# Neighbourhood attention inside a two-layer encoder trunk: a pipeline of tiles, stacked score products, value products of full width

## The chip, the cores and the metric

The kernel runs on one core of one Trainium2 chip. Its engines work side by side: TensorE (PE) multiplies matrices, with a separate record for its weight loads (PEld), VectorE (DVE), ScalarE (ACT) and GpSimd (POOL) work elementwise, and SyncE (SP) starts transfers between the chip's memory and the core. Every engine takes its instructions in the order in which the program lists them. The metric is the device time of one execution in microseconds (us), the median of the runs.

## The reference

The trunk has an even layer (neighbourhood attention beside a gated recurrence) and an odd layer (two other recurrences). Each makes an input projection, its mixers, and an output projection with a residual and a LayerNorm. 2048 tokens stand on a grid of 32 rows of 64. The change touches the attention: each token attends, in 8 heads of 64 channels, to a window of 8 rows and 16 columns.

```
s = jnp.einsum('brnqhd,brnkhd->brnhqk', qb, kg).astype(jnp.float32) * (dh ** -0.5) + bias[None]
s = jnp.where(valid[None, None, :, None], s, -jnp.inf)
p = jax.nn.softmax(s, axis=-1).astype(v.dtype)
o = jnp.einsum('brnhqk,brnkhd->brnqhd', p, vg)
...
ya = ya.reshape(bsz, seq, WIDTH_A) * jax.nn.silu(ag)
...
x = layer_norm(DEEPNORM_ALPHA * x + gate * y, ln_g[l], ln_b[l])
```

All is in 32-bit floats. Products that need the full precision are made of parts: a high part H in the short format (fp32r) and the remainder L, as H·H + H·L + L·H.

## The kernel before

The attention's work is cut into 16 blocks: `rg`, a group of 8 grid rows (512 tokens), by `hp`, a pair of heads. Each block has two heads, each head four tiles `n` of 16 grid columns, so there are 128 tiles of 128 queries. A tile's keys are 24 columns wide at the grid's edges and 32 inside, by 12 grid rows at the top and bottom groups and 16 else: 288, 384 or 512 keys.

`na_block` (L692) writes a block. It fetches q, k and gate for both heads (L702, L704, L706), a bias table for each head (`nat`, L711) and the values (`nav`, L716, one transfer for each of the four widths), and makes high and low parts of q and k (L721 to L724). Then for each head it writes four tiles of scores (three products, `nas`, L741; bias and row minimum on DVE, L744; exponential with row sum on ACT, L746), one reciprocal for the four tiles (L749), and four tiles of values: a scaling on POOL (L754), transposes on PE (`napt`, L757), a copy (`napts`, L760 or L762), and value products (`nay`, L764). At the end of the block comes the gating (`nayo`, L768) and a store.

Both heads of a block share tiles: head h has partitions 64h to 64h + 63 of q and k, so a score product uses 64 of the array's 128 rows; a value product takes 64 of the 128 columns of `nav` as its weights, and so fills 64 of the array's columns.

Around it stand other products. `units` (L1259) writes whole units of the input projection (`oak`, `oav`, `oag` at L204); the last of them are mixed with the first blocks. Then the pool of the input projection is closed, the output projection's weights are fetched, multiplied by a gate and split (`woraw`, `wo`, L783 to L786), and the other blocks alternate with tiles of the output projection (`OutProj.tile`, L826, products `oo` at L860: for each half of the columns and each of 8 chunks, yH·wH, yH·wL, yL·wH).

The final order on each engine is not that of the code: a scheduler simulates the program while it is built and places each instruction when it finds its engine free, by priority (the order of writing). So one engine's list can hold instructions of two or three blocks mixed. The SP queue is part of it: a transfer that waits for a free buffer holds those behind it.

Of the kernel before, what the change touches and what calls it, by code (L numbers as in the profile page):

```python
# [10 lines left out]
F32 = mybir.dt.float32  # L11
# [106 lines left out]
class InProj:  # L118
# [72 lines left out]
    def block(self, u, wh, wl, half, g, i):  # L191
# [4 lines left out]
        for d in range(ND):  # L196
            if u["kind"] == "ch":
                ops = ((wh[:, d, sl], hH[:, d, :]), (wh[:, d, sl], hL[:, d, :]), (wl[:, d, sl], hH[:, d, :]))
                oo = o
            else:  # L200
                ops = ((hH[:, d, sl], wh[:, d, :]), (hH[:, d, sl], wl[:, d, :]), (hL[:, d, sl], wh[:, d, :]))
                oo = o[:, :n]
            for m, (a, b) in enumerate(ops):
                nc.tensor.matmul(oo, a, b, start=d == 0 and m == 0, stop=d == ND - 1 and m == 2)  # L204
        if u["kind"] == "ch":
# [4 lines left out]
    def blocks(self, u, w, half, g):  # L210
        for i in range(u["n"] // P if u["kind"] == "ch" else 4):
            self.block(u, *w, half, g, i)
            yield

# [61 lines left out]
def run(g):  # L276
    for _ in g:
        pass

# [412 lines left out]
def na_block(e, pool, ps, bank, rg, hp, q_d, k_d, v_d, vcol, gate_d, tab_d, y_d):  # L692

    nc = e.nc
    nr = NA_NR[rg]
    nb = nr // 4
    ts_ = slice(rg * 512, (rg + 1) * 512)
    k0 = NA_R0[rg] * 64
    rt = NA_RT[rg]

    q = pool.tile([P, 512], F32, name="naq", tag="naq", bufs=1)
    nc.sync.dma_start(q, q_d[:, ts_])  # L702
    k = pool.tile([P, 1024], F32, name="nak", tag="nak", bufs=1)
    nc.sync.dma_start(k[:, :nr * 64], k_d[:, k0:k0 + nr * 64])  # L704
    gate = pool.tile([P, 512], F32, name="nag", tag="nag", bufs=2)
    nc.sync.dma_start(gate, gate_d[:, ts_])  # L706
    o0, o1 = NA_TOFF[rt, 0], NA_TOFF[rt, 2] + nr * 24
    tabs = []
    for h in range(2):
        t = pool.tile([P, 1280], F32, name="nat", tag="nat", bufs=2)  # L710
        nc.sync.dma_start(t[:, :o1 - o0], tab_d[2 * hp + h, :, o0:o1])  # L711
        tabs.append(t)
    vs = pool.tile([P, 4, 4, P], F32, name="nav", tag="nav", bufs=2)
    vt = v_d[k0:k0 + nr * 64, vcol:vcol + P].rearrange("(b x) d -> x b d", x=256)
    for n in range(4):
        nc.sync.dma_start(vs[:4 * NA_W[n], n, :nb, :], vt[4 * NA_C0[n]:4 * (NA_C0[n] + NA_W[n])])  # L716
    qH = pool.tile([P, 512], F32R, name="qH", tag="qH", bufs=2)
    qL = pool.tile([P, 512], F32R, name="qL", tag="qL", bufs=2)
    kH = pool.tile([P, 1024], F32R, name="kH", tag="kH", bufs=2)
    kL = pool.tile([P, 1024], F32R, name="kL", tag="kL", bufs=2)  # L720
    nc.scalar.copy(qH, q)  # L721
    nc.vector.tensor_sub(qL, q, qH.bitcast(F32))
    nc.scalar.copy(kH[:, :nr * 64], k[:, :nr * 64])
    nc.vector.tensor_sub(kL[:, :nr * 64], k[:, :nr * 64], kH[:, :nr * 64].bitcast(F32))  # L724
    kHv, kLv = (t.rearrange("p (b x) -> p b x", x=256) for t in (kH, kL))
    yp = ps.tile([P, 4, P], F32, name="nay", tag="nay", bufs=e.nay_bufs)
    for h in range(2):
        p0 = 64 * h
        sl = slice(p0, p0 + 64)
        mx = pool.tile([P, 4], F32, name="namx", tag="namx", bufs=3)  # L730
        sm = pool.tile([P, 4], F32, name="nasm", tag="nasm", bufs=3)
        pr = []
        for n in range(4):
            w = NA_W[n]
            nk = nr * w
            off = NA_TOFF[rt, NA_CT[n]] - o0
            sc = bank("nas")
            qs = slice(n * P, (n + 1) * P)
            ks = (slice(0, nb), slice(4 * NA_C0[n], 4 * (NA_C0[n] + w)))
# [3 lines left out]
            p = pool.tile([P, 512], F32, name="nap", tag="nap", bufs=e.nap_bufs)  # L743
            nc.vector.tensor_tensor_reduce(p[:, :nk], sc[:, :nk], tabs[h][:, off:off + nk], -1.0, 3.0e38,  # L744
                                           ALU.add, ALU.min, mx[:, n:n + 1])
            nc.scalar.activation(p[:, :nk], p[:, :nk], AF.Exp, bias=mx[:, n:n + 1], scale=-1.0,  # L746
                                 accum_out=sm[:, n:n + 1])
            pr.append(p)
        nc.vector.reciprocal(sm, sm)  # L749
        for n in range(4):  # L750
            w = NA_W[n]
            nk = nr * w
            p = pr[n]
            nc.gpsimd.tensor_tensor(p[:, :nk], p[:, :nk], sm[:, n:n + 1].broadcast_to([P, nk]), ALU.mult)  # L754
            pt = ps.tile([P, 4, P], F32, name="napt", tag="napt", bufs=e.napt_bufs)
            for b in range(nb):
                nc.tensor.transpose(pt[:4 * w, b, :], p[:, b * 4 * w:(b + 1) * 4 * w], e.ident)  # L757
# [801 lines left out]
```

## Time and profile before

| | |
|---|---|
| median of 3 runs | 2823.4 us (2813.05 to 2828.3) |
| the profiled execution | 2820.02 us |
| its span, first to last instruction | 2818.2 us |
| PE busy | 2584.9 us (92%) |
| DVE, ACT, POOL busy | 1510.3, 1095.2, 1327.7 us |
| mean granted PE clock | 0.951 |

The page gives busy time for each engine and the span in 40 slices of 70.5 us. A busy share counts an engine as busy while a product runs, whatever the clock; the granted clock is a row of its own (1.00 is 2.4 GHz, 0.50 is 1.2 GHz). Window tables cut the span where one likes, timelines list instructions with their start, and wait lists say whom an engine waited for.

### The profile page before, as it was taken

The numbers are of one execution on the slowest core, as the hardware profiler recorded it, in microseconds if no ns is written. First come the engines' busy times: TensorE is split into PE (matmuls) and PEld (weight loads), VectorE is DVE, ScalarE is ACT, GpSimd is POOL, SyncE is SP. The second block draws the span as 40 slices with busy tenths as digits, with TensorE's granted clock in tenths as the row PEclk, the third lists the DMA queues.
The fourth block names the chain that finished last, engine by engine and source line by source line (L and its number), as shares of the span: only waits on it lengthen the run. The fifth ranks groups of instructions, "written<-read, shape, count | busy, mean of one in ns | idle before, by whom it ended". The sixth has DMA issues, their size and how long they took to land. (4 is left out here: it accounts for less than half of the span.)

```text
span 2818.2 us, 53141 instructions
## 1 busy us (share of the span) xinstructions
PE 2584.9 (92%) x21112; PEld 2135.7 (76%) x21112; DVE 1510.3 (54%) x2463; ACT 1095.2 (39%) x2309; POOL 1327.7 (47%) x1289
## 2 busy tenths in 40 slices
PE   7988998988989999999898899999979988889998
PEld 5866778877778767777787777898777767767776
DVE  6255422144433355554546647333565479788886
ACT  3154412244434443433233334423334334655553
POOL 4253323343444243333356556334444577567775
PEclk9999999998999969999999999999999989989999
DMA  8424353322367554645456234443345655734341
GB/s 270 159 76 155 117 172 120 120 78 82 126 192 229 168 173 150 188 139 173 129 162 211 99 120 128 161 138 132 110 138 188 195 174 178 236 125 159 98 138 67
DMA packets 261000, 420.93 MB, mean 149 GB/s; under 512 B 21232, under 2 KB 138896, under 8 KB 260752
## 3 DMA queue, kind: packets, MB, share of 16 engines
q1 hardware_dynamic: 260752, 417.53, 45.9%
q8 instruction: 167, 2.74, 0.4%
q14 instruction: 81, 0.66, 0.1%
HBM read 285.07 MB, written 132.38 MB: 148 GB/s over the span
## 5 line engine op out<-in xcount | busy, mean ns | idle before, releaser
L186 POOL TENSOR_TENSOR wl<-wraw,wh 128x1024 fp32r<-128x1024 f32 (+2 forms) x116 | 292.1, 2535 | 447.6 <-ACT wh L185 436.5
L860 PE MATMUL oo<-wo,yH 128*128 128x512 f32 x1024 | 325.1, 404 | 5.8 <-ACT yH L844 3.3
L860 PEld LDWEIGHTS oo<-wo,yH 128*128 128x128 f32 x1024 | 191.8, 192 | 51.4 <-ACT yH L844 7.9
L754 POOL TENSOR_TENSOR nap<-nap,nasm 128x384 f32<-128x384 f32 (+2 forms) x128 | 115.7, 933 | 177.0 <-DVE nasm L749 175.2
L860 PE MATMUL oo<-wo,yL 128*128 128x512 f32 x512 | 197.9, 401 | 0.6 <-DVE yL L845 0.3
L463 POOL TENSOR_TENSOR Kp<-Kp,T 128x256 f32<-128x256 f32 x144 | 127.3, 889 | 116.1 <-ACT km L422 47.8
L185 ACT CAST wh<-wraw 128x1024 fp32r<-128x1024 f32 (+2 forms) x116 | 116.8, 1051 | 140.4 <-PE oak L204 19.9
L459 DVE TENSOR_TENSOR Q<-Q,T 128x512 f32<-128x512 f32 x144 | 146.0, 1015 | 1.2
L970 DVE SCALAR_TENSOR_TENSOR cva<-cvx,cw,cva 128x512 f32<-128x512 f32 x96 | 104.6, 1097 | 75.1 <-ACT cva L968 73.7
L461 DVE TENSOR_TENSOR Kp<-Kp,T 128x256 f32<-128x256 f32 x144 | 100.2, 696 | 63.8 <-PE l L449 28.9
L764 PE MATMUL nay<-napts,nav 128*64 128x128 f32 (+1 forms) x896 | 131.5, 295 | 1.0 <-ACT napts L762 1.0
L764 PEld LDWEIGHTS nay<-napts,nav 128*64 128x64 f32 (+1 forms) x896 | 103.3, 146 | 32.5 <-issue 22.1
L860 PEld LDWEIGHTS oo<-wo,yL 128*128 128x128 f32 x512 | 96.7, 189 | 25.3 <-DVE yL L845 3.0
L156 POOL TENSOR_TENSOR hL<-hf,hH 128x512 fp32r<-128x512 f32 x36 | 50.1, 1400 | 126.8 <-ACT hH L155 126.7
L746 ACT ACTIVATE nap<-nap,namx 128x384 f32<-128x384 f32 (+2 forms) x128 | 79.3, 620 | 64.9 <-DVE namx L744 63.9
L204 PE MATMUL ox<-hH,wh 128*128 128x512 f32 x256 | 103.5, 404 | 0.3 <-ACT st L310 0.3
L204 PE MATMUL ox<-hL,wh 128*128 128x512 f32 x256 | 103.6, 405 | 0.0
L204 PE MATMUL oqf<-hH,wh 128*128 128x512 f32 x256 | 103.0, 403 | 0.0
L204 PE MATMUL ox<-hH,wl 128*128 128x512 f32 x256 | 103.0, 402 | 0.0
L204 PE MATMUL oqf<-hH,wl 128*128 128x512 f32 x256 | 102.8, 402 | 0.0
L744 DVE CUSTOM_DVE_ANT_0 nap<-nas,nat 128x384 f32<-128x384 f32 (+2 forms) x128 | 70.5, 558 | 58.1 <-PE napt L757 29.9
L204 PE MATMUL oqf<-hL,wh 128*128 128x512 f32 x256 | 101.5, 397 | 0.0
(376 smaller groups left out, 7764.5 us busy)
## 6 DMA issues: line engine op xcount, KB each, us to landing
wraw<-in_o_w_dram SPq DMA_DIRECT2D x56, 512.0 KB
wraw<-in_e_w_dram SPq DMA_DIRECT2D x44, 512.0 KB
adw<-in_ada_w_dram SPq DMA_DIRECT2D x32, 512.0 KB
tk<-xtok SPq DMA_DIRECT2D x31, 384.0 KB
nat<-in_na_tab_dram SPq DMA_DIRECT2D x16, 640.0 KB
xt<-in_x_dram SPq DMA_DIRECT2D x16, 512.0 KB
adw<-in_ada_p_dram SPq DMA_DIRECT2D x16, 512.0 KB
r<-in_x_dram SPq DMA_DIRECT2D x16, 512.0 KB
```

Of the source, the lines that this page charges most:

```text
L185: nc.scalar.copy(h[:, sl], raw)
L186: (nc.vector if e.wl_dve else nc.gpsimd).tensor_sub(l[:, sl], raw, h[:, sl].bitcast(F32))
L204: nc.tensor.matmul(oo, a, b, start=d == 0 and m == 0, stop=d == ND - 1 and m == 2)
L459: nc.vector.tensor_tensor(qv, qv, view(tcur, toff + 1, [[nb - 1, 2], [2, n2], [0, s]]), ALU.mult)
L461: nc.vector.tensor_tensor(kv, kv, view(tcur, toff + nb + 1, [[2, n2], [0, s]]), ALU.mult)
L463: nc.gpsimd.tensor_tensor(kv, kv, view(tcur, toff, [[2, n2], [0, s]]), ALU.mult)
L744: nc.vector.tensor_tensor_reduce(p[:, :nk], sc[:, :nk], tabs[h][:, off:off + nk], -1.0, 3.0e38, ALU.add, ALU.min, mx[:, n:n + 1])
L746: nc.scalar.activation(p[:, :nk], p[:, :nk], AF.Exp, bias=mx[:, n:n + 1], scale=-1.0, accum_out=sm[:, n:n + 1])
L754: nc.gpsimd.tensor_tensor(p[:, :nk], p[:, :nk], sm[:, n:n + 1].broadcast_to([P, nk]), ALU.mult)
L764: nc.tensor.matmul(yp[sl, n, :], vs[:4 * w, n, b, p0:p0 + 64], pts[:4 * w, b, :], start=b == 0, stop=b == nb - 1, tile_position=(0, p0))
L860: nc.tensor.matmul(o, a[:, c, :], b[c][:, ns], start=c == order[0] and m == 0, stop=c == order[-1] and m == 2)
L970: nc.vector.scalar_tensor_tensor(acc, xr[:, k:k + SW], cw[:, i, k:k + 1], acc, ALU.mult, ALU.add)
```

## The change

`na_block` becomes a class `Na` whose `steps` is a generator. It runs over all 128 tiles; at step j it writes the scores of tile j, the transposes of tile j - 3 and the value products of tile j - 4, and yields after each. A head's q, k and table are fetched three tile steps ahead of its first scores. `weave` distributes n of these yields evenly over the steps of another generator: units of the input projection cut into steps of two chunks (`fine`), and output tiles cut into steps of two products (`OutProj.steps`).

For each head, q and k (64 channels) are fetched twice, into both halves of the partitions. `qS` holds the high part of q above and the low part below; with kH and kL, each twice, two products of 128 rows give (qH + qL)·kH + (qH + qL)·kL. The values' weights are all 128 columns of `nav`, both heads'; the half of the output that belongs to the other head is not read. Keys of the tiles with 24 columns and 16 rows are cut into three pieces of 128 instead of four of 96, and `nav` is fetched piece by piece. The reciprocal is made for each tile, the gating for each head. PSUM banks for scores go from 3 to 2, for `nay` from 1 to 2; `yH` of the output projection has 2 buffers in layer 1. Output products run with the low part's products last in each group of chunks, in both layers; in layer 1, for the last tiles of each group of four, both column halves alternate and the last chunk is fetched later (`across`).

```diff
-            for m, (a, b) in enumerate(((qH, kHv), (qH, kLv), (qL, kHv))):
-                nc.tensor.matmul(sc[:, :nk], a[sl, qs], b[sl, ks[0], ks[1]], start=m == 0, stop=m == 2,
-                                 tile_position=(p0, 0))
...
-            for b in range(nb):
-                nc.tensor.matmul(yp[sl, n, :], vs[:4 * w, n, b, p0:p0 + 64], pts[:4 * w, b, :],
-                                 start=b == 0, stop=b == nb - 1, tile_position=(0, p0))
...
+class Na:
+    LAG = (0, 3, 4)
...
+            w4 = 4 * NA_W[n]
+            kb = w4 if b.nb * w4 % P else P
+            b.kb.append(kb)
+            for j in range(b.nb * w4 // kb):
+                at = j * kb
+                while at < (j + 1) * kb:
+                    r, x = divmod(at, w4)
+                    m = min(w4 - x, (j + 1) * kb - at)
+                    nc.sync.dma_start(vs[at - j * kb:at - j * kb + m, n, j, :],
+                                      vt[4 * NA_C0[n] + x:4 * NA_C0[n] + x + m, r])
+                    at += m
...
+        for o in range(2):
+            os_ = slice(64 * o, 64 * o + 64)
+            nc.sync.dma_start(q[os_], b.q[hs, b.ts])
+            nc.sync.dma_start(k[os_, :nk], b.k[hs, b.ks])
...
+        nc.scalar.copy(s.q, q)
+        nc.vector.tensor_sub(s.q[64:], q[64:], s.q[64:].bitcast(F32))
+        nc.scalar.copy(kH[:, :nk], k[:, :nk])
+        nc.vector.tensor_sub(kL[:, :nk], k[:, :nk], kH[:, :nk].bitcast(F32))
...
+        for m, k in enumerate(s.k):
+            nc.tensor.matmul(sc[:, :nk], s.q[:, n * P:(n + 1) * P], k[:, :b.nb, 4 * NA_C0[n]:4 * (NA_C0[n] + w)],
+                             start=m == 0, stop=m == 1)
...
+        for j in range(nj):
+            nc.tensor.matmul(s.yp[:, n, :], b.vs[:kb, n, j, :], s.pts[n][:kb, j, :], start=j == 0, stop=j == nj - 1)
...
+        prods = [(c, m) for cs in (order[:cut], order[cut:]) for ms in ((0, 1), (2,)) for c in cs for m in ms]
...
-    units("ak1 ag0", 1)
-    na(3, 0)
-    units("av1", 1)
-    na(3, 1)
-    units("ag1", 1)
+    units("ag0", 1)
+    weave(na, 36, ip.fine(U["ak1"], 1), ip.fine(U["av1"], 1))
+    weave(na, 24, ip.fine(U["ag1"], 1))
...
-    for rg in (2, 1, 0):
-        for hp in range(4):
-            na(rg, hp)
-            op.tile(4 * (rg + 1) + 3 - hp)
+    for _ in range(36):
+        next(na)
+    for t in range(15, 4, -1):
+        weave(na, 24 if t > 7 else 32, (op.steps(t, *(((3, 4), False, None, True) if t % 4 == 3 else ())), 24))
+    run(na)
+    op.tile(4)
```

PE, among the products of the second output tile, before. Names: `nas` scores, `nay` values, `napt` transposes, `oo` output products; the last field is the output's size and how many stand in a row.

```order
L860 MATMUL oo<-wo_9655,yL 128x512
L741 MATMUL nas<-kH,qH 128x384
L741 MATMUL nas<-kL,qH 128x384
L741 MATMUL nas<-kH,qL 128x384
L764 MATMUL nay<-napts,nav 64x128 x8
L757 MATMUL napt<-c_ident,nap 128x128 x4
L757 MATMUL napt<-c_ident,nap 96x128 x4
L741 MATMUL nas<-kH,qH 128x512
```

PE, in the same part of the stage, after.

```order
L952 MATMUL oo<-wo_9446,yH 128x512
L817 MATMUL nay<-napts,nav 128x128 x4
L799 MATMUL napt<-c_ident,nap 128x128 x3
L785 MATMUL nas<-kL,qS 128x384
L817 MATMUL nay<-napts,nav 128x128 x3
L799 MATMUL napt<-c_ident,nap 128x128 x4
L785 MATMUL nas<-kH,qS 128x512
L785 MATMUL nas<-kL,qS 128x512
L952 MATMUL oo<-wo_9447,yH 128x512
```

Scores are pairs instead of threes, values fill 128 columns, and values, transposes and scores of different tiles follow one another in shorter groups.

SP, at the fetches for a block during the output tiles, before. `nav` is the values, `nat` a table, `naq` and `nak` q and k, `x`, `r` and `y` those of the output tiles and the attention's result.

```order
L704 DMA nak<-ak_77 128x1024
L711 DMA nat<-in_na_tab_dram 128x1280
L877 DMA x_67<-r 128x1024
L716 DMA nav<-av_91 96x4x128
L770 DMA y<-nayo 128x512
L706 DMA nag<-ag_80 128x512
L716 DMA nav<-av_91 128x4x128 x2
```

SP, at such a place, after.

```order
L762 DMA nak<-ak_75 64x1024 x2
L765 DMA nat<-in_na_tab_dram 128x1280
L761 DMA naq<-aq_71 64x512 x2
L746 DMA nav<-av_91 96x128
L746 DMA nav<-av_91 32x128
L824 DMA y<-nayo 128x512
L746 DMA nav<-av_91 64x128 x2
```

The values' four transfers of a block have become up to twenty small ones, q and k four for each head, and most of q and k stand ahead of the values.

## Rows read from the trace of the kernel before

**Rows 1.** The page: granted clock and memory traffic in 40 slices.

```profile
PEclk9999999998999969999999999999999989989999
GB/s 270 159 76 155 117 172 120 120 78 82 126 192 229 168 173 150 188 139 173 129 162 211 99 120 128 161 138 132 110 138 188 195 174 178 236 125 159 98 138 67
```

**Rows 2.** Windows: us, busy PE, PEld, DVE, ACT, POOL, clock, DMA share, GB/s.

```profile
891.00:965.00 74.00, 74.00 (x469) 62.29 (x469) 21.15 (x57) 28.55 (x61) 16.17 (x18) 1.00 0.50 151
965.00:1054.00 89.00, 82.73 (x353) 57.94 (x351) 44.85 (x98) 42.71 (x93) 46.96 (x36) 0.67 0.61 196
1054.00:1379.00 325.00, 323.21 (x1813) 245.93 (x1811) 165.29 (x355) 118.37 (x261) 119.50 (x132) 1.00 0.49 153
...
990.00:1010.00 20.00, 19.87 (x69) 13.98 (x69) 10.18 (x22) 7.50 (x17) 8.40 (x8) 0.50 0.53 156
```

**Rows 3.** PE's longest waits in stretches 2 and 3: us, times, longest.

```profile
PE nas L741 <- DVE namx L744: 3.8, 2, 1.9
...
PE oo L860 <- ACT yH L844: 0.8, 1, 0.8
```

**Rows 4.** PE's timeline in stretch 3: start, us, instructions, count.

```profile
1143.94 0.44 PE L741 MATMUL nas<-kH,qH 64*128 64x384 f32 x1
1144.22 0.34 PE L741 MATMUL nas<-kL,qH 64*128 64x384 f32 x1
1144.40 0.34 PE L741 MATMUL nas<-kH,qL 64*128 64x384 f32 x1
1144.66 1.09 PE L764 MATMUL nay<-napts,nav 96*64 96x128 f32 x8
1145.68 0.66 PE L757 MATMUL napt<-c_ident,nap 128*128 128x128 f32 x4
...
1146.61 0.39 PE L741 MATMUL nas<-kL,qH 64*128 64x512 f32 x1
1146.84 0.39 PE L741 MATMUL nas<-kH,qL 64*128 64x512 f32 x1
```

**Rows 5.** PE's timeline where both heads' scores stand together.

```profile
1087.69 0.45 PE L741 MATMUL nas<-kH,qH 64*128 64x384 f32 x2
1087.97 0.34 PE L741 MATMUL nas<-kL,qH 64*128 64x384 f32 x2
```

**Rows 6.** PE's timeline from transposes to an output product.

```profile
1083.44 1.09 PE L757 MATMUL napt<-c_ident,nap 128*128 128x128 f32 x8
1084.29 0.48 PE L860 MATMUL oo<-wo,yH 128*128 128x512 f32 x1
```

**Rows 7.** PE's timeline in layer 2: a recurrence's products on the full array.

```profile
2406.95 1.06 PE L504 MATMUL po<-v,Sf 128*128 128x128 f32 x8
```

**Rows 8.** Groups of PE by form, 880 to 1390 us: count, busy, mean ns, idle before.

```profile
L741 PE MATMUL nas<-kH,qH 64*128 64x384 f32 x64 | 25.7, 438 | 0.1
...
L741 PE MATMUL nas<-kH,qH 64*128 64x512 f32 x32 | 16.4, 514 | 2.5 <-DVE namx L744 2.4
...
L741 PE MATMUL nas<-kH,qH 64*128 64x288 f32 x32 | 10.9, 402 | 1.9 <-DVE namx L744 1.9
```

**Rows 9.** The values' transfers on SP: ns on the queue, least, median, most.

```profile
L716 SPq DMA_DIRECT2D nav<-av x64: 320/474/1567, 885.7 to 1329.4; - x64
```

**Rows 10.** Groups of DVE by form, 880 to 1390 us: what is made oftener.

```profile
L722 DVE TENSOR_TENSOR qL<-naq,qH 128x512 fp32r<-128x512 f32 x16 | 14.4, 899 | 18.4 <-ACT qH L721 18.3
L724 DVE TENSOR_TENSOR kL<-nak,kH 128x1024 fp32r<-128x1024 f32 x8 | 12.3, 1533 | 0.2
L768 DVE TENSOR_TENSOR nayo<-nay,nag 128x512 f32<-128x512 f32 x16 | 11.0, 688 | 44.5 <-PE nay L764 44.5
...
L749 DVE RECIPROCAL nasm<-nasm 128x4 f32<-128x4 f32 x32 | 5.4, 170 | 6.9 <-ACT nap L746 6.9
```

**Rows 11.** The tail from 2470 us: two of PE's waits, and a window.

```profile
PE oo L860 <- ACT yH L844: 2.5, 4, 1.1
...
2520.00:2560.00 40.00, 39.08 (x203) 32.45 (x202) 36.71 (x52) 23.09 (x62) 30.14 (x30) 1.00 0.44 137
```

More of the change, by code (lines that the diff above doesn't have):

```diff
@@ L189, in loading, with block @@
         return *(t.rearrange("p (d n) -> p d n", d=ND) for t in (h, l)), parts()
-    def block(self, u, wh, wl, half, g, i):
+    def block(self, u, wh, wl, half, g, i, fine=False):
         e, nc, n = self.e, self.e.nc, u["n"]
@@ L208, in block, with blocks, fine, steps @@
             u["evac"](self, half * HALF + g * 512 + i * P, oo)
-    def blocks(self, u, w, half, g):
+    def blocks(self, u, w, half, g, fine=False):
         for i in range(u["n"] // P if u["kind"] == "ch" else 4):
-            self.block(u, *w, half, g, i)
+            yield from self.block(u, *w, half, g, i, fine)
             yield
+    def fine(self, u, half):
+        def steps():
+            w = self.load(u)
+            for g in range(2):
+                yield from self.blocks(u, w, half, g, True)
+        return steps(), 8 * (u["n"] // P if u["kind"] == "ch" else 4)
     def unit(self, u, half):
@@ L278, in run, with weave @@
         pass
+def weave(back, n, *fronts):
+    fronts = [s for f in fronts for s in [f]]
+    steps = sum(k for _, k in fronts)
+    gen = (x for f, _ in fronts for x in f)
+    done = 0
+    for j in range(n):
+        next(back, None)
+        while done * n < (j + 1) * steps:
+            done += 1
+            next(gen, None)
+    run(gen)
 def mix(*gs):
@@ L824, in tiles, with tile, steps @@
             yield
-    def tile(self, t, late=None, last=False, ready=None):
+    def tile(self, *a, **k):
+        run(self.steps(*a, **k))
+    def steps(self, t, late=None, last=False, ready=None, across=False):
         e, nc, pool = self.e, self.e.nc, self.pool
@@ L832, in tile, with fetch @@
         yr = pool.tile([P, c0 if ready is not None else ND, P], F32, name="yr", tag="yr", bufs=2)
-        yH = pool.tile([P, ND, P], F32R, name="yH", tag="yH", bufs=1)
+        yH = pool.tile([P, ND, P], F32R, name="yH", tag="yH", bufs=e.y_bufs)
         yL = pool.tile([P, ND, P], F32R, name="yL", tag="yL", bufs=1)
         order = [*range(c0), *range(c1, ND), *range(c0, c1)]
-        for c, d in ((0, c0), (c1, ND), (c0, c1)):
+        def fetch(c, d):
             if c == d:
-                continue
+                return
             if c == c0 and ready is not None:
@@ L845, in tile @@
             nc.vector.tensor_sub(yL[:, c:d], src, yH[:, c:d].bitcast(F32))
+        fetch(0, c0)
+        fetch(c1, ND)
+        if not across:
+            fetch(c0, c1)
         r = pool.tile([P, D], F32, name="r", tag="xr", bufs=3)
@@ L854, in tile @@
         st = pool.tile([P, 2, 6], F32, name="bst", tag="bst", bufs=2)
[L855 to L863 removed]
+        os, k = {}, 0
+        ops = ((yH, self.wH), (yH, self.wL), (yL, self.wH))
+        cut = ND - (c1 - c0)
+        prods = [(c, m) for cs in (order[:cut], order[cut:]) for ms in ((0, 1), (2,)) for c in cs for m in ms]
+        for x, n in [(x, n) for x in range(24) for n in range(2)] if across else [(x, n) for n in range(2) for x in range(24)]:
+            ns = slice(n * 512, (n + 1) * 512)
+            c, m = prods[x]
+            if x == 0:
+                os[n] = self.bank("oo")
+            nc.tensor.matmul(os[n], ops[m][0][:, c, :], ops[m][1][c][:, ns], start=x == 0, stop=x == 23)
+            k += 1
+            if across and k == 28:
+                fetch(c0, c1)
+            if k % 2 == 0 and k < 48:
+                yield
+            if x == 23:
+                nc.vector.scalar_tensor_tensor(r[:, ns], r[:, ns], ALPHA, os[n], ALU.mult, ALU.add)
+                nc.vector.bn_stats(st[:, n], r[:, ns])
         mv = pool.tile([P, 2], F32, name="mv", tag="mv", bufs=2)
```

178 lines of the change are left out of this document (95 added, 83 removed).

## The prediction

> **What bounds the kernel now.** Read the page's slices first. TensorE (PE) is busy nearly everywhere, and only slice 15 of the 40 shows a granted clock near half speed (tenths, digit 6) [rows 1]. That slice, 987 to 1057 us, lies in the neighbourhood-attention stage, which the change rewrites: its first score product starts at 891 us and its last value product ends at 1379 us. The window table cuts this stage at the places where PE's neighbours change [rows 2]. **Stretch 1**, 891 to 965 us: neighbourhood tiles among input products, PE busy all 74.0 us at clock 1.00. **Stretch 2**, 965 to 1054 us: neighbourhood tiles alone, while the output weights are fetched; PE busy 82.7 of 89 us, but at clock 0.67. The window 990:1010 inside it has PE busy 19.87 of 20 us at 0.50, that is 1.2 instead of 2.4 GHz. **Stretch 3**, 1054 to 1379 us: neighbourhood tiles among output products, PE busy 323 of 325 us at 1.00. VectorE (DVE), the next engine, is busy 165 us there. The wait list agrees: the longest total of PE's waits in stretch 2 is 3.8 us, in stretch 3 it is 0.8 us [rows 3]. So in stretches 1 and 3 the time is the number of products times their spacing, and in stretch 2 it is about that at a low clock. What leaves PE in this stage leaves the time, up to the next bound.
>
> **Spacing, from the timeline at full clock.** A score product of 384 columns with 64 of the array's rows starts 0.18 us after the one before (1144.22 to 1144.40), one of 512 columns 0.23 us after (1146.61 to 1146.84) [rows 4]; I take 0.13 us for 288 columns in proportion. But the step from the first score product to the second takes 0.28, and from the third to the value products 0.26 [rows 4]: each change between products that use half of the array's rows, half of its columns, or all of it costs about 0.09 us more. Between the full-array transposes and a full-array output product there is no such charge: eight transposes and the step to the output product take 0.85 us, 0.106 each [rows 6]. A value product is two passes; eight passes and the step to the transposes take 1.02 us, 0.117 with the change of shape, so 0.11 us a pass [rows 4].
>
> **The change, part by part.** (a) *Scores.* Before, each of 128 tiles has three products with 64 rows; after, two with 128 rows, the high and low parts of q stacked. The groups give 64 tiles of 384, 32 of 512 and 32 of 288 columns [rows 8]. One product fewer a tile is worth 64 x 0.18 + 32 x 0.23 + 32 x 0.13 = 23.0 us. From that comes off what stacking gives up: at 10 places the trace shows score products of both heads starting together ("x2" in one row, two products in the 0.28 us that one takes) [rows 5]. That is 30 products that were already free: 15 x 0.18 + 15 x 0.13 = 4.6 us, so 18.4 us remain. (The Trainium skill, TensorEngine Tiling (Array Packing), Tiling Modes, Key Properties, says that tiles of the array on different rows run in parallel: a rule against this change. The trace agrees at those 10 places and at no other. Had it held for every tile, 192 pairs would have stood against 256 stacked products, and term (a) would be a loss of 64 x 0.18 = 11.5 us instead of a gain of 18.4.) (b) *Changes of shape.* In the PE order of before there are 337 between the stage's first and last product (43, 69 and 225 in the three stretches); after, none, since scores use 128 rows and values 128 columns. 337 x 0.09 = 30.3 us. (c) *Transposes and values.* 448 become 416 of each, because tiles of 24 columns in the middle row groups are cut into three pieces of 128 keys instead of four of 96: 32 x 0.11 + 32 x 0.22 = 10.6 us. That a value product now has 128 columns instead of 64, half of them thrown away, should cost nothing: the nearest row is the recurrence's full-array product, eight passes in 1.06 us, (1.06 - 0.27) / 7 = 0.113 a pass (0.27 being one alone) [rows 7]. Bounds on 832 passes: 0 to +0.01 us each, at most 8 us.
>
> (a) to (c) make 59.3 us at full clock over the whole stage; (d) places them.
>
> (d) *Order.* Weaving moves tiles. By the orders, stretches 1, 2, 3 hold 19, 30 and 79 tiles before and 22, 18 and 88 after, with the same 618 output products in the stage. PE's demand by the spacings above (0.12 us for an input product of 256 columns, 0.23 for one of 512) in stretches 1 and 3 before is 71.0 + 308.8 less 4 for the pairs = 376; it measured 399, so a factor of 1.06. After it is 62.1 + 5.9 (input products that now lie ahead of the first score) + 271.5 = 339.5, times 1.06 = 360: **39 us gone**. Stretch 2 after holds 29 us of PE work: 30 us at full clock, 57 at half. But PE is no longer last there. It moved 89 us x 196 GB/s = 17.4 MB [rows 2]. Stretch 3 moves 49.7 MB [rows 2], of which 12 output tiles, with three transfers of 0.5 MB each, take 18; so a neighbourhood tile is 31.7 / 79 = 0.40 MB, and 0.50 after, since q and k are fetched for each head into both halves of the partitions. 17.4 - 30 x 0.40 + 18 x 0.50 = 14.4 MB: at the 196 GB/s of now 73 us, at the page's fastest slice (270) 53 us [rows 1]. I take 62: the queue must deliver more at once than it does now, though less than its best slice. **27 us gone.** Together 66 us.
>
> (e) *Added work that should hide.* DVE casts q and k for each head: the 16 low parts of q, 14.4 us, and those of k (8 of 1024 columns, 12.3 us, and 8 of 768, about 8) come a second time [rows 10]; with 96 more reciprocals of 0.17 us and 16 more gatings of 0.7 us DVE gains some 60 us in the stage, 41 of it in stretch 3: 165 + 9 more tiles + 41, about 215 of 289 us. PE hides it; without that cover it is 60 us. ScalarE gains about 24 us and is busy less than DVE [rows 2]. On the sync queue (SP) a block's v is 12 to 20 transfers instead of 4, q and k 8 instead of 2. A v transfer holds the queue 0.474 us in the median [rows 9], so a block's v goes from 1.9 to 5.7 to 9.5 us. Behind it wait the next head's q, k and table, hence its scores on PE. By the order, much of q and k stands ahead of v, and the fetch comes three tile steps (3 x 289 / 88 = 10 us) before its use. I book 0; the bound is 9.5 - 1.9 = 7.6 us for each of 11 blocks, 84 us. (f) *Output projection's last stage.* The new product order (low parts last) also holds in layer 2's tail after 2470 us, where the engines' orders differ again; between, they stand as before. PE waits there 2.5 us for yH [rows 11] and less for yL, so at best some 3 us; DVE at 36.7 of 40 us [rows 11] may come in a worse order. I book 0, from -3 to +10.
>
> The profiled execution took 2820.0 us (span 2818.2); less 66 that is 2754. It lies 3.4 us under the median of the runs (2823.4), so I forecast 2757.
>
> **Rivals.** *The queue.* v's transfers hold up the next head by about 3 us a block: 11 x 3 = 33 us come back, 2790. For it: the bound in (e), and 8 MB more in stretch 3, in less time. Against: SP has waits to spare, and PE's order puts output products in between. *More than forecast.* Stretch 2 at full clock and at the fastest slice (53), stretches 1 and 3 without the 1.06: 2754 - 9 - 20 = 2725. For it: full-array products and a pipeline; against: the weights are still fetched there. *Slower, by the clock.* PE's short waits in stretch 2 (3.8 us in two) [rows 3] lie in the one stretch where its clock fell, and with no input or output products between it stayed at 0.50 though busy [rows 2]. If the finer interleaving makes PE wait once a head in stretch 3, the clock falls there too. At the 0.67 of stretch 2 its 289 us become 431, 142 more: 2754 + 142 = 2896. It turns the result below a mean clock of 289 / (289 + 66) = 0.81. Against: output products lie between, and PE waits for nothing there now. *Nothing gained.* The pipeline is no news: PE's waits are already small, and if the last tile's y (heads of one block, read back through memory) sets the pace, or the tail gives back what the stage won, the time stays within 0.5% (14 us, about what a measurement of this kernel can tell from no change).
>
> **How the numbers follow.** Forecast 0.60, queue 0.19, more 0.08, slower by the clock (or the queue at its bound) 0.07, nothing gained 0.06. The range: 2720 from the better case, 2800 from the queue's rival with the tail's 10 us on top; it leaves out the last two cases and a little more. Faster by over 0.5% holds the first three but for the queue's worse part: 0.86; same 0.07; slower 0.07.
>
> **What would show it.** In the profile after: no score or value product in part of the array, two score products a tile at 0.18 us, values at 0.11 us a pass; steps between kinds without the 0.09 us; PE busy nearly all of stretches 1 and 3 at clock 1.00; a stage of about 422 instead of 488 us; all between its end and layer 2's tail as long as before. It is wrong if PE's waits in the stage rise above some 20 us (the rows then name queue or DVE), if value passes need more than 0.12 us, or if the tail after layer 2's last input product changes by over 10 us.

## The result, and the profile after

The changed kernel takes 2843.2 us (median of 6 runs, 2834.8 to 2846.8) against 2820.7 us for the kernel before (6 runs). The ratio is 1.0075, with a 95% interval of 1.0052 to 1.0098: **slower by three quarters of a per cent**, where 2757 us and a gain of 2.4% were forecast. The profiled execution took 2834.8 us (span 2833.0), the fastest of its six, and 14.8 us more than the one of before.

Five marks on PE's timeline say where it went: the first score, the gate's product `adg` (start of stretch 2), the first output product (start of stretch 3), the last value product, and layer 2's last input product `odz`.

| us | before | after | difference | forecast |
|---|---|---|---|---|
| start to first score | 891.0 | 900.0 | +9.0 | +5.9 (counted in stretch 1) |
| stretch 1 | 74.4 | 76.8 | +2.4 | } -45 (with the +5.9: -39) |
| stretch 3 | 324.9 | 316.7 | -8.2 | } |
| stretch 2 | 88.8 | 62.2 | -26.6 | -27 |
| last value to last `odz` | 1071.2 | 1073.1 | +1.9 | 0 |
| tail, to the end of the span | 367.9 | 404.2 | **+36.3** | 0 |

So two things differ from the forecast: stretches 1 and 3 gave back nearly the whole gain that was booked for them, and the tail, in which one product order alone was changed, lost 36 us. Of the 9 us ahead of the first score 3 mean nothing: in the runs below, with the same code ahead of it, it starts between 890 and 903 us.

The windows of after answer to [rows 2]: us, busy PE, PEld, DVE, ACT, POOL, clock, DMA share, GB/s.

```profile
900.00:976.90 76.90, 67.34 (x437) 61.80 (x436) 32.40 (x93) 37.97 (x77) 15.64 (x20) 0.93 0.50 144
976.90:1039.00 62.10, 42.18 (x230) 35.20 (x228) 40.54 (x88) 31.18 (x67) 36.59 (x28) 0.79 0.79 236
1039.00:1355.70 316.70, 292.23 (x1695) 254.55 (x1695) 208.95 (x479) 141.40 (x310) 129.95 (x137) 0.96 0.69 199
```

In stretch 3 PE was busy 323 of 325 us before; now it is busy 292 of 317. The products became fewer, as booked, but PE now stands still for 24 us. Its wait list over the stage (us, times, longest) names what for; before, the entries of [rows 3] were the longest of stretches 2 and 3.

```profile
PE nay L817 <- ACT napts L804: 11.6, 9, 2.5
PE nay L817 <- DVE napts L802: 10.4, 7, 3.4
PE nas L785 <- DVE namx L789: 8.8, 4, 7.2
PE nas L785 <- ACT kH L771: 8.1, 3, 3.4
PE napt L799 <- POOL nap L792: 6.2, 5, 2.5
```

The wait lists name ACT and DVE, though DVE is busy only 209 of 317 us. ACT's own list shows what they wait for. Its longest entry, for DVE's row minimum, was as long before (63.9 us). New are those for q, k and the output tiles' input, all transfers; before, these were 1.9, 0.7 and 6.0 us.

```profile
ACT nap L790 <- DVE namx L789: 57.6, 40, 3.6
ACT qS L769 <- DMA naq<-aq: 48.7, 16, 10.4
ACT kH L771 <- DMA nak<-ak: 47.9, 21, 6.3
ACT yH L926 <- DMA yr<-y: 26.5, 14, 3.5
```

One instance, followed through the timelines of three engines (start, us, engine, line, operation, count, idle time before it and its cause). SP first, then the transposes that the copy shown needs, ACT and PE:

```profile
1098.31 9.98 SPq L746 DMA_DIRECT2D nav<-av  x18
1109.39 0.34 SPq L974 DMA_DIRECT2D x<-r  x1
1109.83 1.20 SPq L762 DMA_DIRECT2D nak<-ak  x2
...
1109.62 0.60 PE L799 MATMUL napt<-c_ident,nap 128*128 128x128 f32 x4
...
1116.65 1.04 ACT L771 CAST kH<-nak 128x1024 fp32r<-128x1024 f32 x1 [4.83 <-DMA nak<-ak]
1117.60 0.58 ACT L804 COPY napts<-napt 128x512 f32<-128x512 f32 x1
...
1117.74 0.44 PE L785 MATMUL nas<-kH,qS 128*128 128x384 f32 x1 [3.44 <-ACT kH L771]
```

Eighteen transfers of v hold the queue for 10 us. k comes behind them, ACT waits 4.8 us for it, and PE waits 3.4 us for ACT's cast. Since ACT takes its instructions in order, a copy of transposed weights (`napts`), which needs no k, stands behind the cast as well: its four transposes had ended at 1110.2, and it starts at 1117.60. For copies by ACT and DVE the list above counts 22.0 us of PE's time.

The wait has a second price. PE's granted clock was 1.00 in the 10 us up to 1118; right behind PE's wait it is 0.51 for 3.4 us (windows), and eight value passes with the step to the transposes take 1.70 us there (PE's timeline, 1119.37 to 1121.07), about twice what they take at full clock.

```profile
1108.00:1118.00 10.00, 6.56 (x40) 5.57 (x39) 4.06 (x13) 3.36 (x9) 4.98 (x5) 1.00 0.78 219
1118.40:1121.80 3.40, 3.40 (x16) 3.15 (x15) 2.62 (x6) 1.19 (x3) 0.00 (x0) 0.51 1.03 247
...
1119.37 1.91 PE L817 MATMUL nay<-napts,nav 128*128 128x128 f32 x8
1121.07 0.85 PE L799 MATMUL napt<-c_ident,nap 128*128 128x128 f32 x3
```

In stretches 1 and 3 the clock was 1.00 before [rows 2] and is 0.93 and 0.96 now. At two levels, 1.00 and 0.50, that is 2 x 0.07 x 76.9 + 2 x 0.04 x 316.7 = 36 us at 0.50, which cost at most half of it, 18 us (an estimate from these windows).

At full clock the spacing came out as read. In this piece [rows 4] is answered: eight value passes and the step to the transposes take 0.89 us (before: 1.02), the last score to the values 0.18 (before: 0.26). No two score products start together any more [rows 5].

```profile
1130.82 0.33 PE L785 MATMUL nas<-kL,qS 128*128 128x384 f32 x1
1131.00 1.05 PE L817 MATMUL nay<-napts,nav 128*128 128x128 f32 x8
1131.89 0.49 PE L799 MATMUL napt<-c_ident,nap 128*128 128x128 f32 x3
```

The work that was added on DVE answers to [rows 10] and came as booked (count, busy, mean ns, idle before): 27.1 us for the low parts of q where 28.8 were booked, 19.8 for the reciprocals where 21.7 were.

```profile
L770 DVE TENSOR_TENSOR qS<-naq,qS 64x512 fp32r<-64x512 f32 x32 | 27.1, 847 | 51.3 <-ACT qS L769 50.8
...
L791 DVE RECIPROCAL nasm<-nasm 128x1 f32<-128x1 f32 x128 | 19.8, 158 | 37.7 <-ACT nap L790 37.0
```

In the tail both PE and DVE execute as many instructions as before, but are busy longer (PE 326.5 instead of 318.0 us, DVE 315.4 instead of 305.9), the granted clock is lower, and both wait longer. The tail, before and after, in the columns of the windows above:

```profile
2450.30:2818.20 367.90, 318.04 (x1518) 257.15 (x1517) 305.91 (x449) 193.82 (x541) 254.47 (x248) 0.94 0.38 124
```

```profile
2428.80:2833.00 404.20, 326.46 (x1518) 268.39 (x1517) 315.39 (x449) 195.17 (x541) 252.99 (x248) 0.90 0.35 113
```

DVE sat idle 62.0 us before and 88.8 after. Its wait for finished output products alone grew by 24.0 us; others grew or shrank (the longest of before, 10.8 us for transposes, is 6.0 now). Before (from 2450 us) and after (from 2429 us):

```profile
DVE r L862 <- PE oo L860: 9.0, 8, 5.3
```

```profile
DVE r L959 <- PE oo L952: 33.0, 21, 4.7
```

`r` is the residual step behind a finished output tile. PE's timeline after shows what it waits for: all 24 products of a half stand in one run, and the recurrence's products (`pin`, then `py` and `pd`) come behind it. The tail has 23 runs of 24 or more output products after and 15 before.

```profile
2601.44 0.71 PE L1133 MATMUL pcb<-bc 128*128 128x128 f32 x4
2602.09 3.94 PE L952 MATMUL oo<-wo,yH 128*128 128x512 f32 x16
2605.87 1.98 PE L952 MATMUL oo<-wo,yL 128*128 128x512 f32 x8
2607.69 1.03 PE L1176 MATMUL pin<-sf,bc 128*128 128x256 f32 x4
```

### The profile page after: what moved, and what is told of

It reads as the page before. It is cut to its first block, busy times and chain, and to the rows that moved or that the text cites. A ratio compares the mean times of both kernels' runs of the same rounds, so it can differ in the third digit from the quotient of the medians.

```text
span 2833.0 us, 53326 instructions
## 1 busy us (share of the span) xinstructions
PE 2526.3 (89%) x20888; PEld 2141.4 (76%) x20888; DVE 1574.4 (56%) x2613; ACT 1119.2 (40%) x2351; POOL 1332.9 (47%) x1289
## 5 line engine op out<-in xcount | busy, mean ns | idle before, releaser
L952 PE MATMUL oo<-wo,yH 128*128 128x512 f32 x1024 | 271.0, 408 | 5.2 <-ACT yH L926 3.8
L817 PE MATMUL nay<-napts,nav 128*128 128x128 f32 (+1 forms) x832 | 125.5, 294 | 23.0 <-ACT napts L804 11.6
L817 PEld LDWEIGHTS nay<-napts,nav 128*128 128x128 f32 (+1 forms) x832 | 117.2, 207 | 33.8 <-ACT napts L804 15.0
L952 PE MATMUL oo<-wo,yL 128*128 128x512 f32 x512 | 139.3, 398 | 0.0
L485 DVE TENSOR_TENSOR Kp<-Kp,T 128x256 f32<-128x256 f32 x144 | 101.1, 702 | 64.3 <-PE l L473 28.8
L446 ACT COPY km<-Kp 128x512 f32<-128x512 f32 x72 | 50.1, 698 | 119.0 <-DVE Kp L485 31.4
```

The lines of the kernel that those rows point to most:

```text
L485: nc.vector.tensor_tensor(kv, kv, view(tcur, toff + nb + 1, [[2, n2], [0, s]]), ALU.mult)
L817: nc.tensor.matmul(s.yp[:, n, :], b.vs[:kb, n, j, :], s.pts[n][:kb, j, :], start=j == 0, stop=j == nj - 1)
L952: nc.tensor.matmul(os[n], ops[m][0][:, c, :], ops[m][1][c][:, ns], start=x == 0, stop=x == 23)
```

## The experiments

Stage and tail are read at the marks above, in one profiled execution of each kernel. The runs of the kernel before beside each group have medians of 2819.7 to 2825.5 us. What one such reading is worth is seen where the stage's code is the same: 455.7 and 461.6 us with v in pieces, 434.1, 435.6, 436.1 and 440.3 with v merged. A difference of two stages is therefore known to some 6 us.

| kernel | run, us | ratio to before (95%) | stage | tail |
|---|---|---|---|---|
| before | 2820.7 | | 488.1 | 367.9 |
| after | 2843.2 | 1.0075 (1.0052 to 1.0098) | 455.7 | 404.2 |
| tail_old_order | 2817.8 | 1.0000 (0.9980 to 1.0021) | 461.6 | 380.0 |
| before_new_tail | 2864.5 | 1.0154 (1.0128 to 1.0180) | 490.3 | 406.5 |
| v_merged | 2816.8 | 0.9994 (0.9974 to 1.0014) | 434.1 | 409.1 |
| qk_one_head_ahead | 2825.4 | 1.0026 (1.0006 to 1.0046) | 454.6 | 400.2 |
| v_merged_old_tail | **2781.0** | **0.9860 (0.9831 to 0.9890)** | 435.6 | 369.1 |
| half_width_values | 2793.9 | 0.9911 (0.9880 to 0.9942) | 452.0 | 369.2 |
| v_four_old_tail | 2787.5 | 0.9895 (0.9862 to 0.9929) | 447.8 | 368.9 |
| before_v_in_pieces | 2828.5 | 1.0030 (1.0008 to 1.0052) | 481.3 | 379.2 |
| low_last_early_chunks | 2813.8 | 0.9956 (0.9938 to 0.9974) | 440.3 | 399.1 |
| low_last_late_chunks | 2789.5 | 0.9873 (0.9839 to 0.9906) | 436.1 | 380.6 |
| values_one_step_later | 2796.7 | 0.9901 (0.9868 to 0.9933) | 432.5 | 380.3 |
| third_score_product | 2801.9 | 0.9914 (0.9885 to 0.9942) | 451.7 | 369.7 |

**The tail: the product order, from both sides.**

> The changed kernel, with layer 2's output products in the old order (H.H, H.L, L.H chunk by chunk); layer 1 keeps the new one. From the end of layer 2's last input product to the end of the span it took 368 us before and takes 404 after. Theory A (the low parts' products last in each group make PE's place in the tail worse): the tail falls to 368 +- 8 us, the run to 2843 - 36 = 2807 us. Theory B (the scheduler draws the tail's order anew whenever anything ahead of it changes, and what it draws differs by some 30 us whatever the order of the products): the tail lies anywhere between 365 and 405, with no reason to be near 368. Theory C (the tail is slow because of what the stage leaves behind, not because of its code): 404 stays.

```diff
+        if e.y_bufs == 1:
+            prods = [(c, m) for c in order for m in range(3)]
```

> The kernel before, with only layer 2's output products in the new order; the attention and all of layer 1 stay as before. Theory A (order of the products): the tail rises from 368 to about 404 us, the run from 2821 to 2857. Theory B (a new draw): anywhere between 365 and 405; if this one stays under 375 while the changed kernel with the old order stays above 390, the order of the products has nothing to do with it. Theory C (what the stage leaves behind): 368 stays, the run 2821.

The edit is the reverse one, in the kernel before. The tail fell to 380.0 us in the first and rose to 406.5 in the second, without the attention having changed there. Theory A holds and C falls, though 380.0 lies 4 us above A's bound: B is right in part. With the old order every tail of the table is 368 to 370 or 379 to 381 us, two draws of the scheduler, and with the new one 400 to 409. The traces show these to be different orders on PE. In v_merged_old_tail, half_width_values and v_four_old_tail PE's instructions of the tail stand in the very order of before, and the tail takes 368.9 to 369.2 us; tail_old_order and before_v_in_pieces have another order, nearly the same in both, and take 380.0 and 379.2; before_new_tail and v_merged share one new order, and take 406.5 and 409.1, with quite different stages ahead. So the tail's time goes with the order that the scheduler writes, and the products' order moved it by 24.2 us (after to tail_old_order), 38.6 (before to before_new_tail) and 40.0 (v_merged to v_merged_old_tail).

**The queue: fewer transfers, or the same ones earlier.**

> The changed kernel, with the values of a width fetched in one transfer where its pieces start at row borders of the grid: 14 instead of 20 transfers a block in the middle row groups, 4 instead of 12 in the outer ones; 112 fewer in the stage, nothing else changed. The stage (first score product to last value product) takes 455.7 us after. Theory Q (the sync queue's time for each transfer stands between a head and its data): 112 x 0.47 us = 53 us less on the queue, of which PE's waits for the copies and for kH (62 us of waits in the stage in all) lose at least half; the stage falls by 20 to 35 us, to 420 to 435. Theory L (it is not the number of transfers: ScalarE and VectorE take the casts of q and k in order, and these wait for data that are asked for only three tile steps ahead): the stage moves by less than 8 us. The rest of the run may move with a new draw of the tail's order.

```diff
+            if kb == w4:
+                nc.sync.dma_start(vs[:w4, n, :b.nb, :], vt[4 * NA_C0[n]:4 * NA_C0[n] + w4])
+                continue
```

> The changed kernel, with q and k of each head fetched one head (four tile steps) earlier into a second buffer each; their casts stay where they are. To make room the copies of the transposed tiles have 3 buffers instead of 4. Number and size of the transfers stay the same. Theory L (casts in ScalarE's and VectorE's order wait for q and k and hold up the copies behind them): ScalarE's waits for naq and nak in the stage fall from 97 us to under 30, PE's waits in the stage from about 62 to under 35, the stage from 455.7 to about 430 us. Theory Q (the queue's time for each transfer): the queue is as full as before, another transfer (v, tables) is late instead; the stage stays within 8 us of 455.7.

```diff
+            ahead(y + 1)
             if y < len(heads):
                 x, h = heads[y]
-                hs[y] = self.head(bs[x], h)
+                hs[y] = self.head(bs[x], h, raw.pop(y))
```

With 112 transfers fewer the stage fell by 21.6 us. (Stretch 3 fell by 28, but its border moved: 18 and 88 tiles stand in stretches 2 and 3 after, 23 and 83 here.) PE's idle time in the stage fell by 10.8 us, and its busy time by as much, for no fewer products (2398 in the windows here, 2362 after). The clock was low for less of the time: by the windows' clocks, an estimate, for 31 us of the stage at 0.50 instead of 62. (In v_merged_old_tail, with the same stage, idle time is 14.6 us less than after and busy time 5.5.) The windows, then ACT's waits for transfers over the stage:

```profile
901.70:975.70 74.00, 68.26 (x471) 62.53 (x470) 34.70 (x91) 41.37 (x80) 19.57 (x22) 1.00 0.55 158
975.70:1047.10 71.40, 47.31 (x266) 39.48 (x265) 48.95 (x106) 38.08 (x81) 40.37 (x30) 0.82 0.91 263
1047.10:1335.80 288.70, 275.46 (x1661) 242.41 (x1659) 198.16 (x464) 135.21 (x297) 126.26 (x135) 0.99 0.71 206
```

```profile
ACT kH L774 <- DMA nak<-ak: 27.8, 15, 5.4
ACT qS L772 <- DMA naq<-aq: 23.5, 10, 4.5
ACT yH L929 <- DMA yr<-y: 16.5, 10, 2.9
```

With the transfers as they were and q and k asked for one head earlier the stage kept its length (454.6). ACT's waits for q and k did shrink, as theory L said, but those for the output tiles' input took their place, and PE waited 19.4 us there:

```profile
ACT yH L948 <- DMA yr<-y: 62.8, 17, 9.2
...
ACT kH L781 <- DMA nak<-ak: 10.2, 5, 6.0
```

```profile
PE oo L974 <- ACT yH L948: 19.4, 5, 6.7
```

Theory L falls, as far as this edit tests it: it also took one buffer from the copies of the transposed tiles, though PE's waits for these copies did not grow (19.5 us, 22.0 after). Q holds: with as many transfers, another one is late. But the queue is not "full", as Q has it: transfers hold it for 256 of the stage's 455.7 us after, 194 of 434.1 with v merged and 100 of 488.1 before; the rest of the time it waits for data or buffers of single entries. The longest of these waits, for the output tiles' finished rows, did not shrink with v merged (32.8 us, then 47.8), so the gain did not come from there. The bytes are the same in all three. One transfer of v holds the queue 0.430 us in the median after (16 to 64 KB each, x256) and held it 0.474 before (144 to 256 KB, x64) [rows 9], so the number counts, not the size:

```profile
L746 SPq DMA_DIRECT2D nav<-av x256: 303/430/1593, 885.0 to 1316.8; - x128
```

(The Trainium skill, SBUF — State Buffer, The DMA setup-cost knee, states that a transfer has a fixed part that does not scale with bytes, of which a few hundred ns are setup and most is completion. The queue's part here fits that setup, 0.43 against 0.47 us for a quarter of the bytes; what completion takes was not read.)

**Both repairs, and a control in the kernel before.**

> The changed kernel with both repairs: the values of a width in one transfer where its pieces start at row borders (112 fewer transfers), and layer 2's output products in the old order. Alone the first took the stage from 455.7 to 434.1 us, the second the tail from 404 to 380. The engines' order behind the stage is now the one of the kernel before. If the two are independent: stage 434, tail 368, the run 2817 - 41 = 2776 us. Rival: the tail's time comes from something else than its order (a stage that ends early, memory traffic), and stays at 380 or more: 2788 to 2817.

> The kernel before, with each of the values' transfers cut by grid row blocks: 16 or 12 a block instead of 4, 160 more in the stage, 75 us more of the sync queue; nothing else. Theory Q1 (each transfer's time on the queue is on the path in any kernel): the stage (488 us) rises by 20 us or more. Theory Q2 (the queue of the kernel before has slack: it waited there 89 us for the values' buffers alone, and nothing waited for it): the stage stays within 6 us; the queue decides only with the changed kernel's transfers of q and k for each head, which are needed soon after they are asked for.

```diff
-        nc.sync.dma_start(vs[:4 * NA_W[n], n, :nb, :], vt[4 * NA_C0[n]:4 * (NA_C0[n] + NA_W[n])])
+        for j in range(nb):
+            nc.sync.dma_start(vs[:4 * NA_W[n], n, j, :], vt[4 * NA_C0[n]:4 * (NA_C0[n] + NA_W[n]), j])
```

The repairs are independent: stage 435.6, tail 369.1, and 2781.0 us for the run, 1.4% (1.1 to 1.7) faster than before and faster than both kernels. In the kernel before, 160 more transfers cost nothing that shows: its stage is 481.3 us, 6.8 less than before (Q2 had said within 6; five tiles moved from stretch 2 into stretch 3), and PE is busy 411.8 of the 413.1 us of its stretches 1 and 3. Q1 falls; the queue waited for a free v buffer as long as ever (89.8 us, the longest entry of SP's list), so the new transfers can have fallen into its other waits, which shrank (for a table's buffer from 63.2 to 48.8 us, for finished rows from 54.4 to 39.7):

```profile
SPq L717 <- PE nay L765: 89.8, 13, 12.3
```

That run is 8.6 us slower than before; the other draw of the tail (379.2) is 11.3 us longer.

> The kernel of v_merged_old_tail with all of a block's values in 4 transfers, as in the kernel before: 80 fewer than there, 38 us of the sync queue; the tiles of 24 columns in the middle row groups are then again four pieces of 96 keys, which is 32 transposes and 32 value products more, 32 x 0.33 = 11 us of PE at most. If the queue still holds up the stage: 434 falls by 10 to 20 us. If PE sets the third stretch by now (it is busy 275 of 289 us): the stage rises by 4 to 11 us.

```diff
-            kb = w4 if b.nb * w4 % P else P
+            kb = w4
```

The stage rose by 12.2 us to 447.8 (by 8 to 14 against the four readings above), where 4 to 11 were expected if PE sets it. The added products show, and a gain from 80 transfers fewer does not: with 144 transfers of v in the stage, their number no longer decides.

**What a change of shape and a score product are worth.**

> The kernel of v_merged_old_tail, with value products that use only their own head's 64 columns of the weights, as in the kernel before; all else stays. By PE's order this makes 242 changes of shape between value products and others in the stage, where there were none. If each costs about 0.09 us as read in the trace of before: 22 us at full clock, some 15 to 22 in the stage, since PE is busy 275 of 289 us in its third stretch: 434 -> 449 to 456, and steps from a value product to a transpose rise from 0.11 to about 0.20 us. Rival (the charge read there is a matter of what the products wait for and not of their shape, or it hides behind the waits of the stage): under 5 us.

```diff
-            nc.tensor.matmul(s.yp[:, n, :], b.vs[:kb, n, j, :], s.pts[n][:kb, j, :], start=j == 0, stop=j == nj - 1)
+            nc.tensor.matmul(s.yp[64 * h:64 * h + 64, n, :], b.vs[:kb, n, j, 64 * h:64 * h + 64], s.pts[n][:kb, j, :],
+                             start=j == 0, stop=j == nj - 1, tile_position=(0, 64 * h))
```

> The kernel of v_merged_old_tail, with a third score product of full height for each tile (the second one twice, so the low part of k counts double): what stacking the parts of q saved, paid again, and nothing else. It adds 64 x 0.18 + 32 x 0.23 + 32 x 0.13 = 23 us of PE at full clock. If PE sets the stage's first and third stretch with these merged transfers: the stage rises by 17 to 23 us. If the waits for copies and transfers set them, the added products fall into these waits (35 us): under 8 us.

```diff
-        for m, k in enumerate(s.k):
+        for m, k in enumerate((*s.k, s.k[1])):
```

Half the columns cost 16.4 us in the stage, 0.068 us for each of 242 changes; the step from values to transposes is 0.203 us in the median of its 75 places, against 0.112 of 82 with v merged. Six values and that step take 0.80 us in this kernel, 0.66 in after (1126.52 to 1127.18):

```profile
1129.89 0.87 PE L820 MATMUL nay<-napts,nav 128*64 128x128 f32 x6
1130.69 0.66 PE L802 MATMUL napt<-c_ident,nap 128*128 128x128 f32 x4
```

(The Trainium skill, TensorEngine Tiling (Array Packing), Tiling Modes, states that a change of the tiling mode drains the engine. This run agrees that a change has a price, 0.09 us; a drain as such it does not show.) The third score product cost 16.1 us (17 to 23 were expected) of the 23 that it adds to PE. So both terms are real, at some 70% of their size, each to within the 6 us of the readings. The rest fell into waits: PE's idle time in the stage is 39.3 us with v merged, 26.7 with half the columns and 35.3 with the third product.

**What the stage still lacks, and which products make the tail long.**

> The kernel of v_merged_old_tail, with the value products five tile steps behind the scores instead of four (two behind the transposes instead of one), one more buffer for the copies between them, and the output tiles one tile step later. PE waits 14.7 us for these copies in the stage there, and some 20 us for other things. If the single step between copy and use is what the stage still lacks against the forecast of 422: it falls from 436 by 8 to 14 us, and PE's waits for napts go under 5 us. Rival (the copies are late because ScalarE and VectorE have fixed orders in which yH, q and k stand ahead; another wait takes their place): within 4 us of 436, with the waits under other names; the tail may be drawn anew, 369 to 380.

```diff
-    LAG = (0, 3, 4)
+    LAG = (0, 3, 5)
```

The stage fell by 3.1 us, but 41 output products (9 us at 0.23 us each) that stood in it now come behind its last value product, so nothing was gained. PE's waits of value products for copies went from 14.7 to 9.8 us, and transposes took over:

```profile
PE napt L802 <- ACT napts L807: 13.0, 6, 4.5
PE napt L802 <- POOL nap L795: 8.7, 8, 2.9
PE nay L820 <- ACT napts L807: 8.2, 3, 4.5
...
PE nay L820 <- DVE napts L805: 1.6, 2, 1.3
```

This is what the rival said. That the copies are late because of ACT's own order is read from the lists, not shown; what would free them was not tried.

> The kernel of v_merged_old_tail, with the low parts' products last in layer 2 only among the first four chunks (those read back from memory); the last four, made by the recurrence just before, keep the old order. Tail with the old order 369 us there, with the new order in all chunks 400 to 409. In PE's order the tail's output products stand in 15 runs of 24 or more with the old order, in 20 to 23 with the new; VectorE waited 9 to 19 us for them with the old, 33 to 36 us with the new. Theory R (long runs: the recurrence's products and the residual's VectorE steps wait behind a run of 24): this order has 19 such runs, so the tail rises to about 390 to 400. Theory D (data: the low part of the last chunks is made last on VectorE, and moving its products shifts the waits): only the last chunks matter, and the tail stays at 369 +- 5.

> The kernel of v_merged_old_tail, with the low parts' products last in layer 2 only among the last four chunks; the first four keep the old order. PE's order has 17 runs of 24 or more output products in the tail. Theory R (long runs): 375 to 385 us, less than the early chunks' variant. Theory D (data of the last chunks): 400 or more, and the early chunks' variant stays at 369.

```diff
-            prods = [(c, m) for c in order for m in range(3)]
+            prods = [(c, m) for ms in ((0, 1), (2,)) for c in order[:cut] for m in ms] + [(c, m) for c in order[cut:] for m in range(3)]
```

This is the edit for the first four chunks; the other one is its mirror. The first four make the tail long (399.1), the last four do not (380.6, the old order's second draw). Theory D falls. R got both values right, but 380.6 is also what the old order alone can take, so the second run can't tell R from no effect. DVE's residual steps behave as R says, first the early chunks', then the late chunks' variant:

```profile
DVE r L964 <- PE oo L957: 27.6, 21, 5.3
```

```profile
DVE r L964 <- PE oo L957: 11.7, 8, 4.3
```

But the number of long runs does not set the time: 15 gave 368 us (before) as well as 380 (tail_old_order), 17 gave 381 and also 370 (third_score_product), 19 gave 399. That early products without a pause for yL leave no gap for the recurrence's products is my reading of PE's order, not shown.

## Why the prediction was wrong, step by step

**The tail (term f): the step that failed most.** It was booked at 0, between -3 and +10 us, from the small waits for yH and yL [rows 11]. It cost 36.3 us, and 38.6 us in the kernel before. The working looked at what the moved products wait for. It did not look at who comes behind them, nor at the scheduler's new order as a whole: a run of 24 products without a gap is 5.6 us (2602.09 to 2607.69) in which the recurrence's products don't start, and DVE's wait for finished output products grew by 24.0 us. The prediction named the busy DVE and priced it at 10. That the engines' order makes the tail long is shown; which step of it does is open. The low clock has a share too, 0.90 instead of 0.94: 2 x 0.10 x 404.2 less 2 x 0.06 x 367.9 = 37 us more at 0.50, at most 18 us of cost by this estimate, and no run parts it from the waits.

**The queue (term e): booked at 0, with the rival at 33 us.** It took 21.6 us of the stage, to some 6 us. (Stretches 1 and 3 are 393.5 us after and 362.8 with v merged, but a part of these 31 us is work that moved into stretch 2, 71.4 instead of 62.2 us.) The mechanism was the rival's, and its chance of 0.19 was too low. A quarter to a half of it is longer busy time of PE, with the clock low, which the rival did not count. The argument against it, that SP has waits to spare, was read in the kernel before, where it was true (before_v_in_pieces); but there q and k were asked for once a block, and after they are asked for once a head, four transfers each, behind up to 20 of v. A slack that is read in the old order is no slack of the new one; and even after, transfers hold the queue for only 256 of 455.7 us, so spare time in sum says nothing of the place where a head's k is needed. That ACT and DVE take casts in order, and so pass a late k on to copies that need none of it, stood nowhere in the working; it is read from the wait lists and the one instance.

**Products and shapes (a to d): right in kind, two thirds in size.** Stretch 2 moved 62.1 us x 236 GB/s = 14.7 MB, where 14.4 were worked out; that it took 62.2 us, as forecast, was luck, since the 62 was a choice between 53 and 73, and with the same code tail_old_order took 64.2. That transfers set it is argued from the rate, not shown. With v merged stretch 3 took 288.7 us, and the forecast has 289, but for 88 tiles and not 83. The third score product and the half-width values paid back 16 us each of the 23 and 22 priced. A value pass came out at the 0.11 us used, though its row of before gives 0.116 without a change of shape and 0.128 with one, not 0.117. The added DVE work (e) has the size booked: DVE is busy 209 us in stretch 3, for which 215 stood.

**The clock.** The rival had 0.67 for all of stretch 3 and 142 us. It came in small: 0.93 and 0.96 in stretches 1 and 3, at most 18 us, and less where PE's waits were shorter (1.00 and 0.99 in v_merged, 0.98 and 0.97 in v_merged_old_tail). The forecast had stretch 3 at 1.00 and gave the waits no second price.

**The sum.** With both causes taken away the runs have a median of 2781.0 us, 24 over the forecast of 2757 and inside its range. (The profiled execution, the fastest of the six, takes 2768.5 us, 14.5 over the 2754 of the sum; the stage has 435.6 us instead of 422.) So the sum comes near the kernel without its two side effects, and still leaves out PE's 39.3 us of idle time in the stage, for which 8.1 stood before. With either one alone the run is 2817 us, level with before; with both it is slower. The range ended at 2800 because it held the queue in full, but the tail with 10 us only. The text named both signs in advance, waits of PE above some 20 us in the stage and a tail that moves by over 10; as chances they were too small.

## What to carry to other kernels

Where a transfer queue is filled in program order, count transfers, not bytes, and count them between a request and its use in the new order; slack seen before says little. A short wait of PE can cost twice, once as idle time and once as a low clock behind it; both stand in the window rows. Where a scheduler writes the engines' order, an edit that looks neutral (the order of products in a sum) can cost as much as the change that it came with gains: test it alone, in the old kernel too. And ask what stands behind a late instruction on each in-order engine, since that, not the late data itself, is what the wait lists name.

## What was not expected of the hardware

A transfer of 16 to 64 KB held the sync queue about as long as one of 144 to 256 KB (0.430 and 0.474 us in the median). And the first score, with the same code ahead of it, started between 889.6 and 902.5 us in eleven profiled executions of the changed kernel and its variants, so a difference of a few us is read between marks, not from the start.
